# Moving the streamed operands of a split-fp32 kernel to other places modulo 512 bytes

## The chip, the cores and the metric

The kernel runs on one core of a Trainium2 chip. The metric is the device time of one execution in microseconds. The kernel before took 1244.25 us (median of 3 runs, 1238.74 to 1244.99).

## The reference, cut to what matters

Two transformer-like blocks over 256 tokens of width 1024. Nearly all the work is products of activations with large fp32 weight matrices:

```python
proj = h @ w_in[l]                        # 8192 columns, then conv / attention / retention mixers
up   = einsum('bsnw,nwd->bsnd', branches, w_branch[l])
x    = x + merged @ w_o[l]
x    = x + memory_attention(h, mem_n, w_xq[l], w_xkv[l], w_xo[l])
x    = x + square(relu(h @ w_up)) @ w_down
# second block: state-space mixer, then latent attention, each followed by
h    = layer_norm(ALPHA * h + mix)
h    = layer_norm(ALPHA * h + (silu(g) * val) @ down)   # g, val = split(conv(h @ up))
```

## The kernel before, in words

**Split products.** Each operand is kept as a hi part, rounded to the type `fp32r`, and a lo part, the rest. A product is three matmuls into the same PSUM bank (`mm3`): hi by hi, hi by lo, lo by hi, in the order lhsT hi / rhs hi, lhsT hi / rhs lo, lhsT lo / rhs hi. Each matmul has a stationary operand, loaded into the array by a weight load, and a moving operand, which streams past it. The weight load of a matmul is issued while the matmul before it streams.

**Weights.** All weight matrices come as 204 chunks of at most 1 MB in the order of use (`chunk_plan`). A chunk is read into the ring `wr` (two slots of 8 KB per partition), ScalarE copies it into the ring `wh` (hi, four slots), VectorE subtracts to give `wl` (lo, four slots). A planner (`Plan`, `tick`, `split_next`) decides while the program is written at which place in each engine's order these steps stand; it looks at modelled times, not at addresses.

**Two forms of product.** In `wstat` the weights are stationary (128 columns, 512 bytes per partition) and the transposed activations stream past them, 256 columns (1024 bytes) per matmul: tiles `ah`/`al` from `new_act`, `br`, `memT`, `cT`. In `xstat` the activations are stationary and weights stream past them, 512 columns (2048 bytes) per matmul, in the tail of some products too; `wmixed` does the same with 256 columns. `ah`/`al`, `memT` and `cT` are used in both forms; `mt`, `oT`, `gT`, `yT` only in `xstat`.

**Places.** Tiles are placed in SBUF by the order in which pools open: DMA scratch (16,384 bytes per partition), constants, `acts`, small pools, the rings of the weights, then one pool per stage; `memT` and `mt` lie in a pool on the right side. Adding up the tile sizes gives these places modulo 512 bytes in the kernel before:

| tile | place mod 512 | minus the place of the weights |
|---|---|---|
| `wh`, `wl` | 288 | 0 |
| `ah`, `al`, `mt`, `memT` | 480 | 192 |
| `cT` (behind a gap of 704), `oT` of the latent attention | 480 | 192 |
| `br`, `gT`, `yT`, `oT` of the memory attention, its `kT`, `qs`, `v` | 288 | 0 |

A weight chunk's slices begin at multiples of 512 bytes in its slot, save in a few narrow chunks: `dt` has 32 columns (128 bytes) per row block, `kvq` 704 columns. Below, the *offset* of a matmul is the place of what streams minus the place of what is loaded next to it, modulo 512. It is 192 for `ah`, `al`, `memT`, `cT` in `wstat`, 0 for `br`, and 320 (that is, minus 192) where weights stream past tiles at 192.

The order of instructions around the change is set by the planner alone. All instructions are recorded under line 284 (the helper `call` of `Lane`), so groups are told apart by tile names.

Of the kernel before, what the change touches and what calls it, by code (L numbers as in the profile page):

```python
# [6 lines left out]
F32 = mybir.dt.float32  # L7
F32R = mybir.dt.float32r
# [8 lines left out]
P = 128  # L17
D = 1024
S = 256
ALPHA = 4 ** 0.25  # L20
NG = 8
RAW, HELD = 2, 4
# [440 lines left out]
        self.sync = Lane(plan, nc.sync, "sp")  # L463


class Kern:
    def __init__(self, nc, tc, a, dbg=None):
        self.at = Plan()
        self.nc, self.tc, self.a, self.dbg = Engines(nc, self.at), tc, a, dbg
        self.plan, _ = chunk_plan()  # L470
        self.nch = len(self.plan)
        self.n_dma = self.n_prep = self.n_half = self.n_get = self.n_done = 0
        self.raw, self.held, self.subs = {}, {}, []
        self.bg = []
        self.floor = 0.0
        self.turns = {}
        self.blocked, self.table = False, None
        self.work = self.skew = 0.0
        self.sums = np.concatenate([[0.0], np.cumsum([len(ks) * max(n, P) * UNIT for _, ks, _, n, _ in self.plan])])

# [334 lines left out]
        self.nc.sync.dma_start(out=t, in_=self.a["prow"][0:1, o + c0:o + c0 + n].to_broadcast([P, n]))  # L815
        return t

    def new_act(self):

        return (self.acts.tile([P, 8, S], F32R, tag="ah", name="ah"), self.acts.tile([P, 8, S], F32R, tag="al", name="al"), [0, 0])  # L820

    def ready(self, act, k, *taus):
        if len(act) == 3:
# [113 lines left out]

    def gap(self, pool, n):

        pool.tile([P, n // 4], F32, tag="gap", name="gap")  # L940

    def pair(self, pool, name, n):
        return tuple(pool.tile([P, n, S], F32R, tag=name + x, name=name + x) for x in "hl")

    def mm1(self, out, lhsT, rhs, start):
        self.nc.tensor.matmul(out, lhsT=lhsT, rhs=rhs, start=start, stop=True, skip_group_check=True)
# [9 lines left out]
    def mixers(self, act):  # L956
        nc, a = self.nc, self.a
        mp, mp_close = self.open("mix")
        br = self.pair(mp, "br", 12)
        gt = Slots(self, mp, "gt", [P, 3, S], F32, 4)  # L960
        r256 = Slots(self, mp, "r256", [P, 256], F32, 6)
        hb = mp.tile([P, 24], F32, tag="hb", name="hb")
# [260 lines left out]
        ap_close()  # L1223
        rp, rp_close = self.open("merged", side="right")
        mt = self.pair(rp, "mt", 8)
        memT = self.pair(rp, "memT", 8)
        gm = self.bcast("mem", self.gb, "gb")
        g_mem = self.spawn(self.mem_norm(gm, memT))
        for m in range(8):
# [27 lines left out]
    def memory(self, x, mt, memT, mt_close):  # L1257
# [4 lines left out]
        oT = self.pair(mp, "oT", 8)  # L1262

        kT = (mp.tile([P, 8, S], F32R, tag="kT", name="kT"), mt[1])
        qs = Slots(self, mp, "qs", [P, 2, 2, S], F32R, 2)

        pTs = [tuple(k[:, 2 * h:2 * h + 2, :] for k in kT) for h in range(4)]
# [423 lines left out]
    def ffn(self, layer, h, act):  # L1691
        nc = self.nc
        pool, close = self.open(f"ffn{layer}")
        gT = self.pair(pool, "gT", 22)
        r512 = Slots(self, pool, "r512", [P, 2, S], F32, 6)

        def col(t):
            c = COLS["fcw"] + 132 * layer + t
            b = COLS["fcb"] + 44 * layer + t
            return lambda j: self.pcol[:, c + 44 * j:c + 44 * j + 1], self.pcol[:, b:b + 1]  # L1700

        def up_out(j):
            def run(pt, t):
                acc = yield from r512.wait()
                gs = [self.taps(acc[:, i, :], pt[:, 256 * i:256 * i + 256], 3, *col(j + 22 * i)) for i in range(2)]
                for g in gs:
                    next(g)
                yield "dve"
                for _ in zip(*gs):
                    pass  # L1710
                self.free(pt)
                yield "act"
                nc.scalar.activation(acc[:, 0, :], acc[:, 0, :], AF.Silu)
                yield "dve"
                nc.vector.tensor_mul(acc[:, 0, :], acc[:, 0, :], acc[:, 1, :])
                yield "act"
                yield from self.split((gT[0][:, j, :], gT[1][:, j, :]), acc[:, 0, :])
                r512.put(acc)
            return run

        tasks = []
        self.wmixed("fu", act, 8, [up_out(j) for j in range(MIXED["fu"][layer])], tasks)
        self.dump(("h1", "h2")[layer], h)
        for j in range(MIXED["fu"][layer], 22):
            self.wstat("fu", act, 8, up_out(j), tasks)
        g_, b_ = self.bcast(f"lfg{layer}", self.gb, "gb"), self.bcast(f"lfb{layer}", self.gb, "gb")
        act = None if layer else self.new_act()
        ps = self.xstat("fd", [2] * 11, self.lhs(gT), [(0, 512), (512, 1024)], tail=TAIL["fd"][layer],
                        before=lambda c: self.until(*tasks[2 * c:2 * c + 2]),
                        after=lambda t, p, got: self.layernorm(t, h, g_, b_, act, p, got))  # L1730
        close()
        return act
# [32 lines left out]
    def attention(self, h, act):  # L1765
        nc = self.nc
        cos, sin = self.cs[:, 0], self.cs[:, 1]
        pool, close = self.open("mla")
        self.gap(pool, 704)
        cT = self.pair(pool, "cT", 5)  # L1770
        krT = pool.tile([P, S], F32, tag="krT", name="krT")
        knT = pool.tile([P, 8, S], F32, tag="knT", name="knT")
        qnT = pool.tile([P, 8, S], F32, tag="qnT", name="qnT")
# [194 lines left out]
    def program(self):  # L1968
        nc, tc, a = self.nc, self.tc, self.a
        cs = []  # L1970

        def pool(name, bufs=1, **kw):
            cm = tc.tile_pool(name=name, bufs=bufs, **kw)
            cs.append(cm)
            return cm.__enter__()

        cp = pool("const")
        self.gb = pool("gb", 2)  # L1980
        self.dram = pool("dram", space=bass.MemoryType.DRAM)
        self.acts = pool("acts")
        cq = pool("small")
        self.tiny = pool("tiny", 4)
        self.tk = Slots(self, pool("tk"), "tk", [P, D], F32, 2)
        self.wraw, self.whi, self.wlo = pool("wraw", RAW), pool("whi", HELD), pool("wlo", HELD)
        pp = pool("ps", space=PSUM)
        self.mm = Slots(self, pp, "mm", [P, 512], F32, 4)
        self.sm = Slots(self, pp, "sm", [P, 512], F32, 4)

        x = cp.tile([P, 2, D], F32, tag="x", name="x")
        self.cst = cst = cq.tile([P, NCST], F32, tag="cst", name="cst")
        self.ones = cp.tile([P, P], F32, tag="ones", name="ones")
        nc.vector.memset(self.ones, 1.0)

        row = self.tk.get()
        o, w = ROWS["mix"]
        nc.sync.dma_start(out=row[0:1, :], in_=a["prow"][0:1, o:o + w])
        halves = [slice(512 * n, 512 * n + 512) for n in range(2)]
        for c in halves:  # L2000
            nc.sync.dma_start(out=x[:, 0, c], in_=a["x"][0:P, c])
        nc.sync.dma_start(out=cst[:, 0:P], in_=a["cst"][:, 0:P])
        self.pump(1)
        nc.sync.dma_start(out=x[:, 1, :], in_=a["x"][P:2 * P, :])
        self.pump()
        nc.sync.dma_start(out=cst[:, P:], in_=a["cst"][:, P:])
        gs = [self.mm.get() for c in halves]
        for pt, c in zip(gs, halves):
            self.mm1(pt, self.ones[0:1, :], row[0:1, c], True)
        self.tk.put(row)  # L2010
        self.pcol = cp.tile([P, NCOL], F32, tag="pcol", name="pcol")
        nc.sync.dma_start(out=self.pcol, in_=a["pcol"])
        self.ident, self.nu, self.ut = (cst[:, CST[n]:CST[n] + P] for n in ("ident", "nu", "ut"))
        self.at.one = cq.tile([1, 2], F32, tag="one", name="one")
        nc.vector.memset(self.at.one, 1.0)
        self.neg1 = cp.tile([P, P], F32, tag="neg1", name="neg1")
        nc.vector.memset(self.neg1, -1.0)
        self.mhalf = cq.tile([P, 2], F32, tag="mhalf", name="mhalf")
        nc.vector.memset(self.mhalf, -0.5)
        self.identb = cp.tile([P, P], BF16, tag="identb", name="identb")  # L2020
        nc.vector.tensor_copy(self.identb, self.ident)

        self.maskb = cp.tile([P, P], BF16, tag="maskb", name="maskb")
        nc.vector.memset(self.maskb, 0.0)
        nc.gpsimd.affine_select(out=self.maskb, in_=self.maskb, compare_op=ALU.is_ge, fill=-1e30, base=0,
                                pattern=[[-1, P]], channel_multiplier=1)

        act = self.new_act()
        self.until(self.spawn(self.rms(0, x, Halves(gs), act), first=True))

        def second():
            yield from self.rms(1, x, Halves(gs), act)
            for pt in gs:
                self.mm.put(pt)

        self.spawn(second(), first=True)
        mt, memT, mt_close = self.mixers(act)
        self.spawn(self.angles(cp))
        act, close = self.memory(x, mt, memT, mt_close)
        act = self.mlp(x, act, close)  # L2040
        act = self.ssd(x, act)
        act = self.ffn(0, x, act)
        act = self.attention(x, act)
        self.ffn(1, x, act)
        self.drain()
        assert self.n_get == self.nch
        for cm in reversed(cs):
            cm.__exit__(None, None, None)
# [21 lines left out]
```

## Time and profile before

| | |
|---|---|
| runs before | 1244.99, 1238.74, 1244.25 us |
| profiled execution | 1244.83 us; span of its instructions 1243.1 us |
| TensorE matmul busy | 1224.7 us of the span (99%), 8468 matmuls |
| VectorE / ScalarE busy | 853.9 us (69%) / 717.0 us (58%) |
| DMA engines | 182 GB/s read from HBM over the span |
[...]

A matmul's end in these records is modelled. What counts is the distance from start to start, the pace: the number of matmuls in a stretch without idle time gives it. A group's mean duration is a steady amount longer than its pace.

### The profile page before, as it was taken

The page shows a single profiled execution, that of the slowest core. Times are in us where ns is not written, and L with a number is a line of the kernel's source. Part 1 is how long each engine was busy: PE and PEld are TensorE (multiplying, and loading weights), DVE is VectorE, ACT ScalarE, POOL GpSimd, SP SyncE. Part 2 cuts the span into 40 slices and gives each one's busy share as a digit, 9 for nine tenths or more (in the row PEclk, how much of TensorE's full clock was granted, in tenths as well). Part 3 has the DMA queues.
Part 4 walks back from the last instruction along what each step waited for, and adds up shares of the span by engine and source line. Part 5 has one row for each costly group of instructions (what it writes and reads, how often), then busy time and mean ns, then how long its engine had stood idle before and what let it go on. Part 6 is the DMA issues. An engine that isn't in the chain of part 4 may idle for free.

```text
span 1243.1 us, 20768 instructions
## 1 busy us (share of the span) xinstructions
PE 1224.7 (99%) x8468; PEld 1120.8 (90%) x8468; DVE 853.9 (69%) x1378; ACT 717.0 (58%) x1181; POOL 53.5 (4%) x85
## 2 busy tenths in 40 slices
PE   7999999999999999999999999999999999999997
PEld 5978999989989998889999898999988888999986
DVE  5666847666746665446787797877765866888853
ACT  5666546446536554335788765666644575666641
POOL 0011000000000000000111201000000000000000
PEclk9999999999999999999999999999999999999999
DMA  7643355546544546524656555555573443455560
GB/s 254 235 167 127 146 196 219 179 156 228 176 152 159 214 172 221 201 106 166 227 190 233 193 174 194 187 172 202 184 259 118 161 181 123 172 197 182 213 256 35
DMA packets 35425, 227.71 MB, mean 183 GB/s; under 512 B 4321, under 2 KB 4993, under 8 KB 11522
## 3 DMA queue, kind: packets, MB, share of 16 engines
q1 hardware_dynamic: 35330, 226.39, 50.8%
q8 instruction: 66, 1.08, 0.4%
q14 instruction: 29, 0.24, 0.1%
HBM read 225.27 MB, written 1.10 MB: 182 GB/s over the span
## 4 chain that ended last, share of the span: by engine, by line
PE 95%; DVE 3%; DMA 1%; issue 0%; ACT 0%; POOL 0%; SPq 0%; POOLq 0%; DVEq 0%; ACTq 0%
PE mm L284 85%; PE sm L284 9%; DVE wl L284 1%; DVE x L284 1%; DMA wr<-wts 0%; DVE tk L284 0%; DMA cst<-cst 0%; POOL rs L284 0%; ACT wh L284 0%; DVE ln L284 0%; DVE al L284 0%; SPq L284 0%; POOLq L2066 0%; ACT r L284 0%; ACT ah L284 0%
## 5 line engine op out<-in xcount | busy, mean ns | idle before, releaser
L284 DVE TENSOR_TENSOR wl<-wr,wh 128x1024 fp32r<-128x1024 f32 (+3 forms) x408 | 479.4, 1198 | 173.7 <-ACT wh L284 173.0
L284 ACT CAST wh<-wr 128x1024 fp32r<-128x1024 f32 (+3 forms) x408 | 403.6, 1029 | 162.4 <-PE mm L284 87.9
L284 PE MATMUL mm<-ah,wh 128*128 128x256 f32 (+1 forms) x1496 | 421.1, 281 | 0.0
L284 PE MATMUL mm<-ah,wl 128*128 128x256 f32 (+1 forms) x1496 | 417.5, 279 | 0.0
L284 PE MATMUL mm<-al,wh 128*128 128x256 f32 (+1 forms) x1496 | 417.4, 279 | 0.0
L284 PEld LDWEIGHTS mm<-ah,wh 128*128 128x128 f32 (+1 forms) x1496 | 283.0, 189 | 1.6 <-issue 1.1
L284 PEld LDWEIGHTS mm<-ah,wl 128*128 128x128 f32 (+1 forms) x1496 | 281.0, 188 | 0.1
L284 PEld LDWEIGHTS mm<-al,wh 128*128 128x128 f32 (+1 forms) x1496 | 280.5, 188 | 0.4
L284 DVE SCALAR_TENSOR_TENSOR r<-mm,pcol,r 128x255 f32<-128x255 f32 (+2 forms) x212 | 86.9, 474 | 38.6 <-ACT r L284 38.6
L284 PE MATMUL mm<-wl,ah 128*128 128x512 f32 (+3 forms) x320 | 106.3, 338 | 3.1 <-DVE wl L284 3.0
L284 PE MATMUL mm<-wh,ah 128*128 128x512 f32 (+3 forms) x320 | 108.6, 345 | 0.0
L284 PE MATMUL mm<-wh,al 128*128 128x512 f32 (+3 forms) x320 | 105.9, 337 | 0.5 <-DVE al L284 0.5
L284 PE MATMUL mm<-wh,gTh 128*128 128x512 f32 x304 | 96.3, 391 | 0.0
L284 PE MATMUL mm<-wh,gTl 128*128 128x512 f32 x304 | 95.6, 389 | 0.0
L284 PE MATMUL mm<-wl,gTh 128*128 128x512 f32 x304 | 95.6, 390 | 0.0
L284 ACT ACTIVATE r<-mm,pcol 128x256 f32<-128x256 f32 x96 | 48.9, 560 | 46.9 <-PE mm L284 46.9
L284 PEld LDWEIGHTS mm<-wl,ah 128*128 128x128 f32 x320 | 60.3, 189 | 10.2 <-DVE wl L284 4.9
L284 PEld LDWEIGHTS mm<-wh,gTl 128*128 128x128 f32 x304 | 57.1, 188 | 11.8
L284 PEld LDWEIGHTS mm<-wl,gTh 128*128 128x128 f32 x304 | 57.1, 188 | 11.8
L284 PEld LDWEIGHTS mm<-wh,gTh 128*128 128x128 f32 x304 | 56.7, 188 | 12.0 <-issue 0.6
L284 PEld LDWEIGHTS mm<-wh,al 128*128 128x128 f32 x320 | 60.3, 189 | 7.0 <-DVE al L284 1.1
L284 PEld LDWEIGHTS mm<-wh,ah 128*128 128x128 f32 x320 | 60.3, 189 | 6.6 <-issue 0.7
(296 smaller groups left out, 1581.8 us busy)
## 6 DMA issues: line engine op xcount, KB each, us to landing
wr<-wts SPq DMA_DIRECT2D x186, 1024.0 KB, 4.9
wr<-wts SPq DMA_DIRECT2D x11, 768.0 KB, 4.3
gb<-prow SPq DMA_DIRECT2D x12, 512.0 KB, 6.8
dec<-rows SPq DMA_DIRECT2D x8, 768.0 KB, 7.5
wr<-wts SPq DMA_DIRECT2D x4, 704.0 KB, 4.2
wr<-wts SPq DMA_DIRECT2D x4, 512.0 KB, 7.0
tk<-mem SPq DMA_DIRECT2D x2, 512.0 KB, 7.9
out<-x SPq DMA_DIRECT2D x4, 256.0 KB, 2.1
```

Source lines behind the costliest of these rows:

```text
L284: r = f(*args, **kw)
```

## The change

`PLACE = (448, 320)`: hi and lo parts of operands that stream past weights are put 448 and 320 bytes (mod 512) behind the place of the weights. This is done with padding: `new_act` allocates 128 columns more and slices; `stream` replaces `pair` for `br`, `memT`, `cT` and puts gap tiles around them. A gap of 192 bytes ahead of the weights' rings moves these from 288 to 480, so that everything in stage pools without a gap now stands at the weights' own place: `mt`, `oT`, `gT`, `yT`, and the activation for `kvq` (`new_act(False)`). In the memory attention a gap of 64 puts `qs` and `v` 64 bytes behind `kT` and `mt`, which stream past them: offset 448. The DMA scratch shrinks from 16 KB to 1 KB, which makes the room. No instruction is added, removed or resized.

```diff
+PLACE = (448, 320)
...
-    def new_act(self):
-
-        return (self.acts.tile([P, 8, S], F32R, tag="ah", name="ah"), self.acts.tile([P, 8, S], F32R, tag="al", name="al"), [0, 0])
+    def new_act(self, stream=True):
+
+        h, l = (self.acts.tile([P, 8 * S + 128], F32R, tag=n, name=n)[:, (at if stream else 0) // 4:][:, :8 * S]
+                .rearrange("p (k s) -> p k s", s=S) for n, at in zip(("ah", "al"), PLACE))
+        return (h, l, [0, 0])
...
     def gap(self, pool, n):
 
-        pool.tile([P, n // 4], F32, tag="gap", name="gap")
+        self.n_gap += 1
+        pool.tile([P, n // 4], F32, tag=f"gap{self.n_gap}", name="gap")
...
+    def stream(self, pool, name, n):
+
+        self.gap(pool, PLACE[0])
+        h = pool.tile([P, n, S], F32R, tag=name + "h", name=name + "h")
+        self.gap(pool, (PLACE[1] - PLACE[0]) % 512)
+        t = h, pool.tile([P, n, S], F32R, tag=name + "l", name=name + "l")
+        self.gap(pool, -PLACE[1] % 512)
+        return t
...
-        br = self.pair(mp, "br", 12)
+        br = self.stream(mp, "br", 12)
...
-        memT = self.pair(rp, "memT", 8)
+        memT = self.stream(rp, "memT", 8)
...
+        self.gap(mp, 64)
         qs = Slots(self, mp, "qs", [P, 2, 2, S], F32R, 2)
...
-        act = None if layer else self.new_act()
+        act = None if layer else self.new_act(False)
...
-        self.gap(pool, 704)
-        cT = self.pair(pool, "cT", 5)
+        cT = self.stream(pool, "cT", 5)
...
-        self.wraw, self.whi, self.wlo = pool("wraw", RAW), pool("whi", HELD), pool("wlo", HELD)
+        self.gap(pool("gap0"), 192)
+        self.wraw, self.whi = pool("wraw", RAW), pool("whi", HELD)
+        self.wlo = pool("wlo", HELD)
...
-    nc = bacc.Bacc("TRN2", target_bir_lowering=False, num_devices=1)
+    nc = bacc.Bacc("TRN2", target_bir_lowering=False, num_devices=1, dynamic_dma_scratch_size=1024)
```

The offsets after: `wstat` 448 when a hi part streams (two of three passes), 320 when a lo part does; `xstat` and `wmixed` past tiles that also stream 64 and 192; past all others 0.

## Rows read from the trace of the kernel before

**Rows 1.** The page: span, busy time by engine, the granted clock in 40 slices, the chain that ended last by engine.
```profile
span 1243.1 us, 20768 instructions
PE 1224.7 (99%) x8468; PEld 1120.8 (90%) x8468; DVE 853.9 (69%) x1378; ACT 717.0 (58%) x1181; POOL 53.5 (4%) x85
...
PEclk9999999999999999999999999999999999999999
...
PE 95%; DVE 3%; DMA 1%; issue 0%; ACT 0%; POOL 0%; SPq 0%; POOLq 0%; DVEq 0%; ACTq 0%
```

**Rows 2.** PE alone in stretches that hold one kind of product: start and end in us, length, busy time and number of matmuls (those that reach over an edge count too), granted clock, DMA share, GB/s. 236 to 244 is `br`; 500 to 540 is `gT` with 512 columns; the others are `ah`/`al` or (274 to 294) `memT` with 256 columns.
```profile
28.00:44.00 16.00, 16.00 (x138) 1.00 0.61 215
142.00:180.00 38.00, 38.00 (x337) 1.00 0.59 208
236.00:244.00 8.00, 8.00 (x69) 1.00 0.52 187
274.00:294.00 20.00, 20.00 (x174) 1.00 0.58 211
400.00:460.00 60.00, 60.00 (x512) 1.00 0.54 193
500.00:540.00 40.00, 40.00 (x179) 1.00 0.51 185
796.00:890.00 94.00, 94.00 (x800) 1.00 0.53 181
1080.00:1165.00 85.00, 85.00 (x753) 1.00 0.54 186
```

**Rows 3.** Groups of PE by shape: the lo pass of `al` in 1080 to 1165 and in 795 to 890, and `gT` (hi) in 500 to 540. Count, busy us, mean ns of one, idle.
```profile
L284 PE MATMUL mm<-al,wh 128*128 128x256 f32 x251 | 69.4, 276 | 0.0
L284 PE MATMUL mm<-al,wh 128*128 128x256 f32 x270 | 76.0, 281 | 0.0
L284 PE MATMUL mm<-wh,gTh 128*128 128x512 f32 x60 | 18.5, 389 | 0.0
```

**Rows 4.** The timeline of PE at the chunk `dt` (first and last lines; 24 matmuls whose weight loads are 32 columns): start, busy, instruction.
```profile
570.99 0.28 PE L284 MATMUL mm<-ah,wh 128*32 128x256 f32 x1
571.10 0.28 PE L284 MATMUL mm<-al,wh 128*32 128x256 f32 x1
571.22 0.28 PE L284 MATMUL mm<-ah,wl 128*32 128x256 f32 x1
571.34 0.28 PE L284 MATMUL mm<-ah,wh 128*32 128x256 f32 x1
571.45 0.28 PE L284 MATMUL mm<-al,wh 128*32 128x256 f32 x1
...
573.61 0.28 PE L284 MATMUL mm<-ah,wl 128*32 128x256 f32 x1
573.72 0.28 PE L284 MATMUL mm<-ah,wh 128*128 128x256 f32 x1
```

**Rows 5.** The timeline of PE where weights of 512 columns stream past `ah`/`al` (offset 320), first and last line of ten.
```profile
640.70 0.40 PE L284 MATMUL mm<-wh,ah 128*128 128x512 f32 x1
...
642.81 0.40 PE L284 MATMUL mm<-wh,ah 128*128 128x512 f32 x1
```

**Rows 6.** The whole run by shape: the groups that the change touches.
```profile
L284 PE MATMUL mm<-ah,wh 128*128 128x256 f32 x1488 | 418.9, 281 | 0.0
L284 PE MATMUL mm<-ah,wl 128*128 128x256 f32 x1488 | 415.3, 279 | 0.0
L284 PE MATMUL mm<-al,wh 128*128 128x256 f32 x1488 | 415.2, 279 | 0.0
...
L284 PE MATMUL mm<-wh,al 128*128 128x512 f32 x144 | 57.3, 398 | 0.5 <-DVE al L284 0.5
...
L284 PE MATMUL mm<-wh,al 128*128 128x256 f32 x144 | 40.2, 279 | 0.0
...
L284 PE MATMUL mm<-brh,wl 128*128 128x256 f32 x96 | 27.2, 283 | 0.0
...
L284 PE MATMUL mm<-memTl,wh 128*128 128x256 f32 x64 | 17.7, 277 | 0.0
...
L284 PE MATMUL mm<-cTl,wh 128*128 128x256 f32 x40 | 11.1, 278 | 0.0
...
L284 PE MATMUL mm<-wh,mtl 128*128 128x512 f32 x32 | 10.6, 393 | 0.0
...
L284 PE MATMUL sm<-kT,qs 128*128 128x256 f32 x32 | 6.3, 280 | 0.0
...
L284 PE MATMUL mm<-wh,ah 128*128 128x384 f32 x16 | 5.4, 336 | 0.0
```

**Rows 7.** The chain in order of time, the longest pieces without a break in the second and third large stages of `wstat` (start, length, what).
```profile
794.54 154.47 PE mm L284 x1110
1073.74 161.40 PE mm L284 x1158
```

**Rows 8.** What PE waited for: total us, times, longest.
```profile
PE sm L284 <- DVE tk L284: 3.1, 1, 3.1
PE mm L284 <- DVE wl L284: 3.0, 3, 2.0
PE mm L284 <- DMA tk<-prow: 2.4, 1, 2.4
```

More of the change, by code (lines that the diff above doesn't have):

```diff
@@ L477, in __init__ @@
         self.blocked, self.table = False, None
+        self.n_gap = 0
         self.work = self.skew = 0.0
```

## The prediction

> **What bounds the kernel now.** [...] What PE waited for adds up to some 10 us, most of it at the start [rows 8]. So time is matmuls times pace, and the question is the pace.
>
> The pace comes from stretches without a break. A stretch of length T holds n matmuls of which the first reached in from outside, so pace = (T + mean duration) / n. With 256 columns streaming there are three values [rows 2, 3]: (85.00 + 0.276) / 753 = 113.3 ns; (94.00 + 0.281) / 800 = 117.9 and, likewise, 117.8 in 400 to 460 and 118.0 in 28 to 44; (8.00 + 0.283) / 69 = 120.0 for `br`. With 512 columns, past `gT`: (40.00 + 0.389) / 179 = 225.6 by the count, 226 to 227 ns as one or two matmuls over the edge are allowed for: twice 113.3, to within that. The mean duration is the pace plus 163 ns each time (276, 281, 283, 389), so means of groups can be read as paces: clean is 276.5 at 256 columns (69.4 us / 251) and 389 at 512.
>
> What sets the value? Offset 0 with 256 columns (`br`): always 120. Offset 192: 113.3 in 142 to 180, 274 to 294 and 1080 to 1165, 117.8 in 28 to 44, 400 to 460 and 796 to 890 [rows 2]. The last of each are the same code at the same addresses in the two feed-forward layers. So the place doesn't decide the pace alone: at 192 two paces are open, and something at the entry of an unbroken chain picks one, which then holds for 60 to 100 us. Offset 320 with 512 columns gives (642.81 - 640.70) / 9 = 234.4 ns at its worst [rows 5] against 227 at offset 0. At `dt` the weight loads are a quarter as wide; after a few matmuls the pace is (573.72 - 571.45) / 20 = 113.5 ns, while the offset runs through 192, 64, 448 and 320 as the narrow slices move on by 128 bytes [rows 4]. So 113.3 is where the stream itself ends up when the load hardly disturbs it, and 4.5 or 6.7 ns more is what load and stream do to each other.
>
> **The change part by part.** No instruction comes or goes; the planner's order depends on modelled times and not on addresses, so I take the order as unchanged. The sum is made against the profiled execution, 1244.8 us (span 1243.1), 0.6 above the median of the runs.
>
> [...]
>
> *Activations past weights, 192 to 448 / 320.* 3 x 1488 = 4464 matmuls [rows 6]. The lo pass is never the first of a chain, so its mean holds no waits: 415.2 / 1488 = 279.0, against 276.5 clean: 2.5 ns. Times 4464: 11.2 us over the clean pace. (With the means of all three passes, 281.5, 279.1, 279.0, it is 15 us; the difference sits in the pass that starts chains and holds waits.) What will the pace be at 448? No 128-column load at 448 is in the trace. [...] At 448 itself there are only the `dt` rows, at 113.5, with narrow loads; 320 at 256 columns has a mean of 279 [rows 6], in between. I take 113.3, the pace that most offsets can reach: gain 11.2.
>
> *`br`, 0 to 448 / 320.* 3 x 96 matmuls, 27.2 / 96 = 283.3: 6.8 ns above clean, 2.0 us. [...]
>
> *`memT`, `cT` and the heads of the memory attention.* 192 at 0.5 ns, 120 at 1.5, 96 at 3.5 to 5.5 [rows 6]: 0.1 + 0.2 + 0.4 = 0.7 us.
>
> *Weights past `mt` and the latent `oT`, 320 to 0.* 96 + 96 matmuls at 393 against 389 at offset 0 [rows 3, 6]: 0.7 us. Here the row for the new place is in the trace.
>
> *Weights past tiles that also stream, 320 to 64 and 192.* 3 x 144 with 512 columns at 398 and 3 x 144 with 256 at 279, and some 140 past `memT` and `cT`. The only rows with 64 are half of `kvq`, where 384 columns take 336, that is 173 ns against 1.5 x 113.3 = 170: not clean, no worse than 320. I take 0. Bounds: all clean, 432 x 9 + 432 x 2.5 + 140 x 5 = 5.7 us gained; all at the worst rows (234.4 and 120), 432 x 4.2 = 1.8 us lost, and about 1 more with 512 columns.
>
> *DMA scratch, gap tiles, other waits on a tile's room.* Nothing on the path that I can see; POOL issues no DMA, and PE's waits are 10 us in all, so this is bounded by a us or two.
>
> *Is the gain passed on?* VectorE and ScalarE must make weights faster. They do so now: 1158 matmuls from 1073.74 run without a break at 113.3, as the 1110 from 794.54 do at 117.8 [rows 2, 7]. That cover is there in the dense stages; without it the gain of the slow ones would turn into waits for `wl`.
>
> Sum: 11.2 + 2.0 + 0.7 + 0.7 = 14.6 us; 1244.8 - 14.6 = 1230.2, say **1230 us**. With the bounds of the fifth part and the 15 instead of 11.2 it is 1220 to 1236.
>
> **The rivals.**
> *Two paces stay.* 448 / 320 may, like 192, leave two paces open, drawn anew at each entry. Then only `br` and the 0.7 are sure: about 1242, and by how the stretches of 60 to 110 us fall (one of 100 us is worth 100 x 4.5 / 117.8 = 3.8 us) 1236 to 1250. For it: the two feed-forward layers. Against: at offset 0 there is one pace only, so some places fix it.
> *No effect of place.* Load and stream never meet, and the three paces have another cause, such as the other engines' traffic: 1244.8. The equal code of the two layers with its two paces leaves a little room for that; `br`, at 120 in every stretch, little. [...]
> *The new place is worse.* The hi part stands 64 bytes from offset 0, the one place where the pace is always slow. [...] All at 117.8: the mean pace of activations past weights is now 279.0 - 163 = 116.0, so 4464 x 1.8 = 8.0, less 0.6 for `br`, plus 312 x 4 = 1.2 for `memT` and `cT`: 1253. Hi passes at 120 and lo passes at 117.8, mean 119.3: 4464 x 3.3 = 14.7, `br` 0.2 less, the others 1.7 more: 1261. It decides from a mean pace of 116.0 on; `dt`, clean at 448 itself, speaks against, and so do the clean 512-column rows at offset 0.
> [...]
>
> **How the numbers follow.** Clean pace nearly everywhere: 0.48, 1220 to 1236. Two paces stay: 0.24. No effect: 0.03. Worse: 0.16, half of it below 1256. Below 113.3: 0.09. Differences within 0.5%, about 6 us, can hardly be told from no change: that is 1238 to 1250.5. Faster: 0.48 + 0.09 + 0.03 of the second case = 0.60; same 0.21 + 0.03 = 0.24; slower 0.16. The range 1220 to 1256 holds 0.48 + 0.27 + 0.08 = 0.83; the likeliest case alone has 1220 to 1236.
>
> **What would show it.** Right: in the stretches of `up` and both feed-forward layers the mean of all three passes is 276 to 277; `br` falls from 283 to 276; past `mt` 389; PE's waits don't grow. Wrong: a mean of 281 or 283 in any long stretch (two paces, or the worse place), a mean under 275 (below 113.3), or new waits of PE for `wl` where the pace did fall. The prediction falls if the hi passes stay within 3 ns of the 283 that `br` had before.

## The result: 1.0% slower, and the profile after

The changed kernel takes 1254.03 us (median of 4 runs, 1253.90 to 1254.29), the kernel before 1242.45 beside it (4 runs, 1238.74 to 1244.99): a ratio of 1.0096, 95% interval 1.0066 to 1.0125. The time lies inside the range, but it moved to the other side: 14.6 us of gain were forecast, and 9.2 to 11.6 were lost (by the spans of the profiled executions and by the medians).

The page of the kernel after: span, busy time, granted clock, the chain that ended last by engine, and what PE waited for (total us, times, longest).
```profile
span 1252.3 us, 20769 instructions
PE 1234.3 (99%) x8468; PEld 1128.8 (90%) x8468; DVE 854.4 (68%) x1378; ACT 716.7 (57%) x1181; POOL 53.2 (4%) x85
...
PEclk9999999999999999999999999999999999999999
...
PE 93%; DVE 3%; DMA 1%; issue 1%; POOL 0%; ACT 0%; SPq 0%; POOLq 0%; DVEq 0%; ACTq 0%
```
```profile
PE mm L284 <- DVE wl L284: 3.2, 4, 1.9
PE mm L284 <- DMA tk<-prow: 2.4, 1, 2.4
PE sm L284 <- DVE tk L284: 2.3, 1, 2.3
```
Against [rows 1, 8] the span is 9.2 us longer, and PE's busy time 9.6 (1234.3 against 1224.7) for the same 8468 matmuls at the same granted clock (0.998 on average in both). Waits are as before. The loss is in the pace alone, so it is read from stretches without a break and from the means, as in the prediction.

PE of the kernel after in stretches of one kind of product (start and end in us, length, busy, number of matmuls, clock, DMA share, GB/s): gates, `br`, `up`, `gT`, both feed-forward layers.
```profile
142.00:180.00 38.00, 38.00 (x325) 1.00 0.58 199
236.00:244.00 8.00, 8.00 (x70) 1.00 0.65 219
400.00:460.00 60.00, 60.00 (x512) 1.00 0.54 197
500.00:540.00 40.00, 40.00 (x178) 1.00 0.55 195
800.00:890.00 90.00, 90.00 (x767) 1.00 0.51 177
1080.00:1160.00 80.00, 80.00 (x682) 1.00 0.52 183
```
With the working of the prediction the paces are (38 + 0.281) / 325 = 117.8 ns, (8 + 0.281) / 70 = 118.3 for `br`, then 117.7 in `up` and in both feed-forward layers. The gates and the second layer stood at 113.3 before [rows 2]: the stretches that were clean no longer are, those at 117.8 stay there. Weights past `gT`, whose offset stays 0, keep their pace: 178 matmuls in 40 us for 179, a mean of 389 ns before and after.

Whole-run groups of PE after the change (count, busy us, mean ns of one, idle).
```profile
L284 PE MATMUL mm<-ah,wh 128*128 128x256 f32 x1488 | 420.7, 283 | 0.0
L284 PE MATMUL mm<-al,wh 128*128 128x256 f32 x1488 | 418.3, 281 | 0.0
L284 PE MATMUL mm<-ah,wl 128*128 128x256 f32 x1488 | 416.6, 280 | 0.0
...
L284 PE MATMUL mm<-wh,al 128*128 128x512 f32 x144 | 57.1, 397 | 0.5 <-DVE al L284 0.5
...
L284 PE MATMUL mm<-wh,al 128*128 128x256 f32 x144 | 39.9, 277 | 0.0
...
L284 PE MATMUL mm<-brh,wl 128*128 128x256 f32 x96 | 26.9, 280 | 0.0
...
L284 PE MATMUL mm<-memTl,wh 128*128 128x256 f32 x64 | 18.1, 282 | 0.0
...
L284 PE MATMUL mm<-cTl,wh 128*128 128x256 f32 x40 | 11.3, 282 | 0.0
...
L284 PE MATMUL mm<-wh,mtl 128*128 128x512 f32 x32 | 10.5, 390 | 0.0
```
The largest group rose where it should have fallen (281 for `ah` past `wh`, 279 for the other two before [rows 6]), `memT` and `cT` rose by 4 to 5 ns, `br` fell by 3, `mt` by 3, and `wmixed` (weights of 256 columns past activations) by 2.

From the distances start to start one can add up how far each class lies above the clean pace. That pace is taken as 113.3 ns for 256 columns and in proportion for other widths (226.7 for 512); distances are cut off at 7.5 ns more, so that waits don't count, and products that are not split are left out. In us:

```
class                                before   after
activations past weights (ah, al)     11.65   19.86
br                                     1.84    1.27
memT                                   0.11    0.83
cT                                     0.21    0.56
weights of 512 past ah, al             1.69    2.21
weights of 256 past ah, al (wmixed)    1.75    0.65
weights past mt                        0.27    0.12
all split products                    20.28   28.18
```
The whole is 7.9 us of the 9.2, and `ah` and `al` alone lose 8.2 in the term that was to give 11.2. Without the cut-off the sum over all distances is 9.2 us, 9.1 of it where `ah` and `al` stream.

### The profile page after: what moved, and what is told of

Its sections match the earlier page's. It is cut to its first block, busy times and chain, and to the rows that moved or that the text cites. A ratio compares the mean times of both kernels' runs of the same rounds, so it can differ in the third digit from the quotient of the medians.

```text
span 1252.3 us, 20769 instructions
## 1 busy us (share of the span) xinstructions
PE 1234.3 (99%) x8468; PEld 1128.8 (90%) x8468; DVE 854.4 (68%) x1378; ACT 716.7 (57%) x1181; POOL 53.2 (4%) x85
## 4 chain that ended last, share of the span: by engine, by line
PE 93%; DVE 3%; DMA 1%; issue 1%; POOL 0%; ACT 0%; SPq 0%; POOLq 0%; DVEq 0%; ACTq 0%
PE mm L284 84%; PE sm L284 9%; DMA wr<-wts 1%; DVE wl L284 1%; DVE x L284 1%; DVE tk L284 0%; POOL rs L284 0%; DVE ln L284 0%; SPq L284 0%; DVE al L284 0%; ACT wh L284 0%; ACT ah L284 0%; POOLq L2083 0%; ACT r L284 0%; DVEq L2083 0%
```

## The experiments

The question is what about (448, 320) is worse than 192. The theory: a hi and a lo place fix the pace as a pair, through how the stream and the weight load beside it meet. Its rivals: being near offset 0, the sign of the distance, the moved weights or the smaller DMA scratch, or luck at the entries. Six kernels measure paces alone; the others are the whole kernel with other places. In the tables below an *excess* is (pace in ns x 2.4) minus the columns, from the tenth matmul of a chain to its last (the granted clock is 1.00 in all of them): for 256 columns 16 is 113.3 ns, 26.6 is 117.8, 32 is 120.0. The factor 2.4 only makes a scale, whose unit is called a cycle in one of the expectations; no run here shows how long a cycle of the clock is.

### The pace by place, 64 pairs

A kernel that holds only chains of 12 x 3 matmuls (12 triples, a triple being the three matmuls of one split product); every chain has its own pair of places and one of three things ahead of it, its *entry*:
```diff
+        for h, l in COMBOS:                      # 0, 64 .. 448 each
+            for kind in ("transposes", "wide", "both"):
+                enter(kind)
+                ...
+                for k in range(12):
+                    ...
+                    mul(o, wh[:, w], ah[:, sh], k == 0, False)     # sh starts at h bytes
+                    mul(o, wh[:, w], al[:, sl], False, False)      # sl at l bytes
+                    mul(o, wl[:, w], ah[:, sh], False, k == 11)
```


> A kernel of its own, which leaves out the whole computation: chains of 36 matmuls in the order of the split product (weights stationary with 128 columns, 256 columns streaming past), no other engine at work, for all 64 pairs of places of the hi and the lo part (0 to 448 in steps of 64 bytes, relative to the weights), each entered in three ways: behind four transposes, behind three matmuls with 512 columns, behind both. Theory 1, place: the pace is set by the pair alone or by pair and entry; (448, 320) gives 117.8 ns at every entry, (192, 192) 113.3 or 117.8 by entry, (0, 0) 120, and some pairs give 113.3 at every entry. Theory 2, traffic: with no other engine at work all pairs run at one pace, 113.3.

The timeline of PE in three chains, (256, 256), (448, 320) and (448, 448): the tenth matmul and the last of each, 26 apart.
```profile
559.06 0.28 PE L48 MATMUL mm<-ah,wh 128*128 128x256 f32 x1
...
562.18 0.28 PE L48 MATMUL mm<-ah,wl 128*128 128x256 f32 x1
...
934.97 0.28 PE L48 MATMUL mm<-ah,wh 128*128 128x256 f32 x1
...
938.03 0.28 PE L48 MATMUL mm<-ah,wl 128*128 128x256 f32 x1
...
965.03 0.28 PE L48 MATMUL mm<-ah,wh 128*128 128x256 f32 x1
...
967.98 0.28 PE L48 MATMUL mm<-ah,wl 128*128 128x256 f32 x1
```
(562.18 - 559.06) / 26 = 120.0 ns, as `br` had at 0. (448, 320): (938.03 - 934.97) / 26 = 117.7. (448, 448): (967.98 - 965.03) / 26 = 113.5, with times rounded to 10 ns. So the three paces of the kernel before are there with VectorE and ScalarE idle and 1 GB/s of DMA beside PE (the page of this run, from its second slice to its last). The excess of the quarter of the table that is enough (the other three repeat it: adding 256 to either place changes nothing beyond 1, or 0.4 ns, save for the first chain of the program, whose first matmuls are slower (213 ns from start to start between 14.81 and 16.09 us), and one entry at (192, 0)), for the three entries:

```
hi \ lo      0              64             128            192
  0       - /32/32     26.6/26.6/26.6  26.1/26.6/26.6  26.7/26.7/26.9
 64    29.0/30.0/30.0  26.6/26.7/26.6  26.5/26.5/26.5  26.6/26.6/26.6
128    31.1/29.4/29.4  23.9/23.8/24.8  29.0/29.0/32.0  35.5/26.6/33.9
192    30.3/26.6/26.6  26.6/26.6/26.6  29.3/29.4/28.8  16.0/26.6/16.0
```
The period is 256 bytes and not 512, so 448 is 192 and 320 is 64. For the activations the change kept the hi parts where they had been, and moved only the lo parts, from a pair that has two paces to one that has the slow one alone. Which of its two paces that pair takes goes by the entry here: at all four pairs that are (192, 192) modulo 256 it is the clean one behind transposes and behind both, the slow one behind the wide matmuls.

### The same with 512 columns

```diff
-                    mul(o, wh[:, w], ah[:, sh], k == 0, False)
+                    mul(o, ah[:, sh], wh[:, w], k == 0, False)     # w: 512 columns
```
(and so for the other two; eight triples, two entries).

> The same with the roles turned, which again leaves out the whole computation: the 128-column tiles stationary at the 64 pairs of places, 512 columns of weights streaming past at place 0, 24 matmuls a chain, entered behind four transposes or behind six matmuls with 256 columns. Theory 1: (0, 0) gives 226.7 ns, (192, 192) 229 to 234, (448, 320) 229 to 234 with a pattern over the three passes. Theory 2: all pairs at 226.7.

Only (0, 0) is clean there (excess 32, 226.7 ns); all others lie at 37 to 52 (229 to 235 ns), (192, 192) at 37.3 to 37.9, (192, 64) at 37.3. It repeats after 256 bytes too, though some entries at (0, 192), (128, 0) and (192, 0) differ by 2 to 4 (0.8 to 1.7 ns). So of these places the form with weights streaming is fastest at offset 0, where the form with activations streaming takes 32 (120.0 ns), near the slow end; that form is clean at (192, 192) alone.

### The pair mirrored, and the pair of before

```diff
-PLACE = (448, 320)
+PLACE = (64, 192)
...
-        self.gap(mp, 64)
+        self.gap(mp, -PLACE[0] % 512)
```


> The whole kernel with hi and lo parts at 64 and 192 in place of 448 and 320: the same distances to the other side. In the changed kernel, weights with 256 columns streaming past tiles at 448 and 320 see just these offsets, 64 and 192, and run clean there. Theory 1 with the sign as the cause: activations past weights fall from a mean of 281 to about 276.5, 5184 matmuls by 4.4 ns, so 1254 - 23 = 1231 us, give or take 3 for the weights that now stream past tiles at offsets 448 and 320. Rival, any place near 0 is bad: mean 281 to 283, 1252 to 1262. Rival, place is not the cause: 1254.

1253.47 us (5 runs, 1252.81 to 1253.97), a ratio of 1.0067 to the kernel before, 1.0044 to 1.0091 (1243.77 in 8 runs beside it). Its stretches of `up` and the two feed-forward layers:
```profile
400.00:460.00 60.00, 60.00 (x512) 1.00 0.54 197
800.00:890.00 90.00, 90.00 (x766) 1.00 0.51 178
1080.00:1160.00 80.00, 80.00 (x682) 1.00 0.51 182
```
The 1231 us of the first theory didn't come. The counts are those of the change to within one, as 26.6 at (64, 192) in the table says. For this pair the sign plays no part; that it never does isn't shown, and in the table (64, 64) is slow at every entry where its mirror (192, 192) is not.

The same two lines with `PLACE = (192, 192)`: the weights, the gaps and the DMA scratch of the change, and the offset of `ah` and `al` before, now for `br` as well.

> One part of the change alone: the weights and all that does not stream move as in the change, and so do br and cT, but everything that streams stands at 192, hi and lo, as the activations did before. Theory 1: two paces again, 1236 to 1246 us with a spread over the runs like before, br at 276 or 281 instead of 283. If it is as slow as the change (1254 with little spread), not the places 448 and 320 but something else in the change (DMA scratch, gaps) costs the time.

1236.72 us (4 runs, 1236.18 to 1236.81), 0.993, 0.9905 to 0.9955. What the change does besides choosing its pair costs nothing, and with `br` at 192 it gives a little. The wide spread that was expected didn't come: the runs lie within 0.6 us. Two of its stretches, slow and clean:
```profile
28.00:44.00 16.00, 16.00 (x138) 1.00 0.64 232
...
400.00:460.00 60.00, 60.00 (x532) 1.00 0.59 211
```

### One number of the change undone

```diff
-PLACE = (448, 320)
+PLACE = (448, 448)
```


> The changed kernel with one number changed: lo parts at 448 instead of 320. Modulo 256 the pair is then (192, 192) instead of (192, 64). If the pace has a period of 256 bytes and the pair decides, the two paces come back: 1236 to 1246 us, long stretches at a mean of 276 or 281 ns, none held at 281 everywhere. If the place of the hi part at 448 was the fault, or 448 is not the same as 192, the time stays at 1254.

1235.9 us (7 runs, 1235.55 to 1236.75), 0.9966, 0.9955 to 0.9978 (1240.56 in 16 runs beside it). Its stretches and groups:
```profile
28.00:44.00 16.00, 16.00 (x138) 1.00 0.62 225
...
236.00:244.00 8.00, 8.00 (x73) 1.00 0.52 157
...
400.00:460.00 60.00, 60.00 (x532) 1.00 0.59 208
...
800.00:890.00 90.00, 90.00 (x797) 1.00 0.55 196
1080.00:1160.00 80.00, 80.00 (x708) 1.00 0.55 198
```
```profile
L284 PE MATMUL mm<-ah,wh 128*128 128x256 f32 x1488 | 415.7, 279 | 0.0
L284 PE MATMUL mm<-ah,wl 128*128 128x256 f32 x1488 | 412.2, 277 | 0.2 <-DVE wl L284 0.2
L284 PE MATMUL mm<-al,wh 128*128 128x256 f32 x1488 | 412.1, 277 | 0.0
...
L284 PE MATMUL mm<-wh,al 128*128 128x256 f32 x144 | 40.2, 279 | 0.0
```
532 for 512, 797 for 767, 708 for 682: the place of the lo part alone is worth 1254.0 - 1235.9 = 18 us (16 by the two ratios to the kernel before). As with (192, 192), the time came out at the lower end of what was expected, with little spread. The hi part still stands at 448, 64 bytes from offset 0, so nearness to 0 isn't the cause; and as (448, 448) takes the time of (192, 192), the period of 256 holds in the whole kernel. `wmixed` is back at the 279 of before: the 2 ns that it gained came from the lo part's new place.

### Luck at the entries

In 72 entries (0 to 5 transposes and 0 to 5 wide matmuls, in both orders) for each of three pairs:
```diff
-ENTRIES = ("transposes", "wide", "both")
+ENTRIES = [(t, w, o) for t in range(6) for w in range(6) for o in (0, 1)]
...
-COMBOS = [(h, l) for h in range(0, 512, 64) for l in range(0, 512, 64)]
+COMBOS = [(192, 192), (192, 64), (0, 0)]
```


> What picks the pace (leaves out the whole computation): chains of 36 narrow matmuls at the pairs (192, 192), (192, 64), (0, 0), entered behind 0 to 5 transposes and 0 to 5 wide matmuls in either order. (192, 64) stands for the change, 448 and 320 being 192 and 64 modulo 256. Theory 1: (0, 0) at 120 ns and (192, 64) at 117.8 at every entry, (192, 192) at 113.3 or 117.8 by entry and at nothing else. If entry is what decides at every place, (192, 64) also shows 113.3 somewhere, and the change was only unlucky.

(192, 192) behind two transposes and one wide matmul, in the one order and in the other; the tenth matmul and the last:
```profile
142.04 0.28 PE L48 MATMUL mm<-ah,wh 128*128 128x256 f32 x1
...
144.99 0.28 PE L48 MATMUL mm<-ah,wl 128*128 128x256 f32 x1
...
146.61 0.28 PE L48 MATMUL mm<-ah,wh 128*128 128x256 f32 x1
...
149.67 0.28 PE L48 MATMUL mm<-ah,wl 128*128 128x256 f32 x1
```
2.95 / 26 = 113.5 ns and 3.06 / 26 = 117.7. Of all entries:

(192, 64): 27 at all 72. (0, 0): 32 at all 72. (192, 192): 16 at 37 of them, 27 at 34, nothing between (the program's first chain is left out). Without transposes ahead, all ten entries behind wide matmuls took the slow pace; with transposes it was 36 clean to 24 slow, and no rule in their number that I could find. In a later sweep, below, (192, 192) took the clean pace behind three wide matmuls, so what stood further ahead counts too. The chains that end clean reach it by the sixth matmul; the others are slow to their end. Two paces, picked in the first matmuls of a chain and held, are thus a property of that pair and not of the stage or of the other engines. That the runs of the kernel before spread over 6 to 8 us and those of the change over 0.4 would fit this, as the change has nothing to draw, but it isn't shown: one execution of each kernel has a trace, and the two kernels with (192, 192) and (448, 448) can draw too and spread over 0.6 and 1.2 us.

A last kernel is the kernel before with every tile 192 bytes further on, all offsets kept:
```diff
+        self.gap(pool("gap0"), 192)
         cp = pool("const")
...
         memT = self.pair(rp, "memT", 8)
+        self.gap(rp, 320)
...
```


> The kernel before with every tile moved on by 192 bytes mod 512 (gap of 192 ahead of the constants, one of 320 behind memT in the pool on the right, DMA scratch 1 KB); every offset of the kernel before stays as it was: 192 for ah, al, memT, cT, 0 for br, 320 past mt and oT. Theory A (only offsets count, the pace at 192 is drawn anew at entries, and what is at 0 or 320 costs the same): ratio 0.998 to 1.002, runs spread over 1238 to 1246 like the kernel before, some long stretches at 117.8 ns. Theory B (the two kernels with (192, 192) and (448, 448) ran steadily at 1236 because their tiles stand at other absolute places): runs within 1 us of each other, at 1238 to 1239.5 (1236 and 2.7 us for br, mt and oT), the long stretches all at 113.3 ns.

1240.25 us (12 runs, 1238.82 to 1246.96) against 1240.39 (17 runs, 1238.47 to 1246.56): 0.9998, 0.9981 to 1.0015. Theory A holds; this move of the absolute place counts for nothing, median and spread are the same. Its draw in the profiled execution:
```profile
28.00:44.00 16.00, 16.00 (x144) 1.00 0.68 244
...
400.00:460.00 60.00, 60.00 (x512) 1.00 0.56 202
...
800.00:890.00 90.00, 90.00 (x767) 1.00 0.53 188
1080.00:1160.00 80.00, 80.00 (x708) 1.00 0.54 196
```
Clean at 28 to 44, where the kernel before drew the slow pace (138 [rows 2]), and otherwise the same draws. What stays open is why the two kernels with both parts at 192 or 448 run so steadily (11 runs within 1.3 us). In their traces the long stretches are clean, while 28 to 44 is slow in both (138 matmuls). Their `br` stands at 192 instead of 0, so that no stretch at 120 ns lies among the others; whether that is what steadies them wasn't tried.

### Looking for a pair without the draw

Steps of 16 bytes, modulo 256, with 10 triples and two entries:
```diff
-COMBOS = [(h, l) for h in range(0, 512, 64) for l in range(0, 512, 64)]
+COMBOS = [(h, l) for h in range(0, 256, 16) for l in range(0, 256, 16)]
```


> The narrow sweep again (it leaves out the whole computation), now over 256 bytes in steps of 16, as the first sweep repeated itself every 256 bytes: 256 pairs, chains of 30 matmuls, entered behind four transposes and behind three wide matmuls. If only the distance to the nearest bad place counts, the paces between the steps of 64 lie between those of their neighbours and no place is clean at both entries. If the pattern is finer, some pairs are at 113.3 ns (16 cycles over 256) at both entries, and the kernel can be placed so that no entry falls into the slow pace: by the counts of before, some 11 us less than 1243.

Most of the 256 pairs lie between 24 and 33 (116.7 to 120.4 ns) and nothing can be interpolated: neighbours of a slow pair are now slower, now faster. (112, 112) alone is clean (17) at both entries, (0, 0) is at 32. So the whole kernel with `PLACE = (112, 112)`:

> The changed kernel with hi and lo parts at 112, the pair that was clean at both entries of the sweep in steps of 16 bytes. If the sweep holds in the whole kernel, all activations past weights run at a mean of 276 to 277 ns at every entry: the 6.4 us that the kernel with 192 still loses there are gone, 1230 us, give or take 2 for weights streaming past tiles at 112, which no sweep has shown, and with a small spread. If the places of the weights' slots or other engines matter as well, some stretches are at 281 and it lands at 1236 to 1245.

1241.1 us (10 runs, 1240.38 to 1243.05), 0.9997, 0.9983 to 1.0011. No gain where 1230 was expected; two stretches and two groups of it say why:
```profile
236.00:244.00 8.00, 8.00 (x69) 1.00 0.45 158
...
400.00:460.00 60.00, 60.00 (x532) 1.00 0.54 194
```
```profile
L284 PE MATMUL mm<-al,wh 128*128 128x256 f32 x1488 | 410.5, 276 | 0.0
...
L284 PE MATMUL mm<-wh,al 128*128 128x256 f32 x144 | 40.8, 283 | 0.0
```
`ah` and `al`, each a slice of a wider tile, are clean: 276. But tiles of their own were put at multiples of 32 bytes, so a gap of 112 left `br` at 128 (69 matmuls in 8 us, as at offset 0) and `mt` 32 bytes off its place (395 and 400 ns). And `wmixed`, now past tiles at 112, rose from 279 to 283.

One more measurement of paces: 50 entries at (112, 112) and at (192, 208), and both parts together in steps of 8 bytes, for both forms of product:
```diff
+        for h in range(0, 256, 8):
+            ...
+                    s = slice(h // 4 + 256 * q, h // 4 + 256 * q + 128)
+                    mul(o, ah[:, s], wh[:, w], k == 0, False)
```


> Chains alone (leaves out the whole computation): the pairs (112, 112) and (192, 208) behind 50 entries each; then equal places from 0 to 248 in steps of 8, with 512 columns streaming at two entries and with 256 columns at three. If (112, 112) is clean whatever the entry, all 50 chains are at 113.3 ns; if the sweep only met two lucky entries, some are at 117.8. With 512 columns only places near 0 should be at 226.7.

(112, 112) lies at 16 to 19 at 49 entries (the fiftieth is the program's first chain): most of its chains start slower, all come to the clean pace by the 16th matmul and lie at 16 over their last ten. (192, 208) lies at 24 to 25, at 32 at one entry. Of the 32 places of both parts together, 16, 112, 144 and 192 reach 16 to 18 at some entry, only 112 at all of them. With 512 columns not only 0 is clean, as was expected, but 120 and 216 too (16 and 240 at one entry); 112 has 48, 192 has 37.

Then everything streamed at exactly 112 by slices, only the state-space mixer's activation at 192:
```diff
-PLACE = (448, 320)
+PLACE, SSD = 112, 192
...
+    def placed(self, pool, name, n, at=PLACE):
+
+        return tuple(pool.tile([P, n * S + 128], F32R, tag=name + x, name=name + x)[:, at // 4:][:, :n * S]
+                     .rearrange("p (k s) -> p k s", s=S) for x in "hl")
...
-        br = self.stream(mp, "br", 12)
+        br = self.placed(mp, "br", 12)
...
```


> All that streams past weights at exactly 112 (tiles with 128 columns of room and a slice, as separate tiles can only be placed in steps of 32 bytes), save the activations of the state-space mixer, past which many wide matmuls stream, at 192; all else at the weights' place as in the change. br, memT and cT fall from a mean of 282 to 284 (in the kernel with 112) to 276 to 277: 1.3 + 0.9 + 0.6 us; mt and the latent oT return to the clean 389: 1 us; so 1241.1 - 3.8 = 1237, less 0.6 for the mixer. If 192 was only lucky in its entries, this is the steadier one at 1235 to 1237; if the wide matmuls at 112 cost more than they seem to, 1238 to 1241.

1236.75 us (7 runs, 1235.02 to 1238.55), 0.9954, 0.9937 to 0.9972: where it was expected, and no better than (448, 448).
```profile
L284 PE MATMUL mm<-al,wh 128*128 128x256 f32 x1488 | 410.3, 276 | 0.0
...
L284 PE MATMUL mm<-wh,al 128*128 128x256 f32 x144 | 40.8, 283 | 0.0
L284 PE MATMUL mm<-brh,wh 128*128 128x256 f32 x96 | 26.6, 277 | 0.0
```
The long passes and `br` are clean. The sums over the clean pace, made for both kernels as above, say why that brings nothing over (448, 448): 1.4 us are gained with `ah`/`al` streaming and 0.7 with `memT`, and 0.7, 0.6 and 0.3 lost with weights past `ah`/`al` (256 and 512 columns) and past `memT`. What streams in one product stands still in another, and the two forms want different places.

### Does the load take part? Loads of 32 columns

```diff
-                    w = slice(256 * q, 256 * q + 128)
+                    w = slice(256 * q, 256 * q + 32)
```
(and the products go to 32 partitions of PSUM instead of 128).

> The narrow sweep over 64 pairs with the suspected cause taken down to a quarter: weight loads of 32 columns instead of 128, the streams unchanged (it leaves out the whole computation). If load and stream meeting in SBUF is what costs the time, most pairs are at 113.3 ns, the others nearer to it than with 128 columns, (0, 0) and (192, 64) among them. If the stream's own place against something else decides, the table stays as it was: 120 at (0, 0), 117.8 at (192, 64).

The tenth matmul and the last at (256, 256), 120.0 ns with full loads, now (559.22 - 556.16) / 26 = 117.7:
```profile
556.16 0.28 PE L48 MATMUL mm<-ah,wh 128*32 128x256 f32 x1
...
559.22 0.28 PE L48 MATMUL mm<-ah,wl 128*32 128x256 f32 x1
```

The streams stand where they stood, only the load is a quarter as wide: (0, 0) falls from 32 to 27 at most entries, (192, 64) from 26.6 to 23, (192, 192) from two paces to 16 at all three entries, (64, 64) from 26.6 to 16 at two entries and 24 at one. Most pairs lie at 21 to 27, so neither expectation came true as it stood: only 29 of the 192 chains are at 16, and the table changed nearly everywhere. Of the chains 157 got faster by more than 1, and only those at (128, 64) slower (24 or 25 to 27). So loads of 32 columns, with products on 32 partitions, mostly lessen the loss but don't take it away. Where in the chip it arises, and why some pairs pay more than others, no run shows.

## Why the prediction was wrong, point by point

**What bounds the kernel: right.** Time is matmuls times pace: PE is busy 99% of the span before [rows 1] and after, at a granted clock of 1.00 in all stretches above and in [rows 2]. The order of PE's matmuls is that of before, its waits didn't grow [rows 8], and PE's busy time grew by 9.6 us where the span grew by 9.2.

**Three paces, two of them open at 192, drawn at entry: right.** All three came out of a kernel with nothing else at work, to 0.2 ns, and the draw with them. The rival that place has no effect falls: one shape at one clock takes 113.3, 117.8 or 120.0 ns with nothing but the places and the entries changed, and with a narrower load 157 of 192 chains are faster.

**Activations past weights at 448 / 320 take 113.3 ns, gain 11.2 us: the step that failed.** They take 117.8 everywhere and the term is a loss of 8.2. The prediction's own sign of its fall came true: hi passes within 3 ns of the 283 that `br` had, now at 283 and 280. Two things were wrong in it. The only rows at 448 were those of `dt` [rows 4], whose loads are 32 columns, and I let them stand for loads of 128. Moreover hi and lo stand alike in `dt`, at 192 and then at 64 modulo 256. The runs show that with such loads these two pairs take 16, or 24 at one entry, and the change's mixed pair, (192, 64), takes 23; with full loads it takes 26.6. The reading of `dt` as "where the stream ends up when the load hardly disturbs it" is half right (some pairs do reach 16), but what it was to prove is not in it. And I took the two numbers one by one, modulo 512 as the kernel's text has it. Modulo 256 they are 192 and 64: the hi part hadn't moved, so that the only question was the lo part's 64, for which the trace had next to nothing (half of `kvq` in the other form [rows 6], and the 234.4 ns of [rows 5]). The trace of before could not show the period; it did show that there was no row for the pair, and 0.48 for the clean pace was too much for a price that rested on `dt`.

**"The new place is worse", all at 117.8: this is what happened**, with its price. It said 8.0 for `ah` and `al`, less 0.6 for `br`, plus 1.2 for `memT` and `cT`, 1253 us. Measured are 8.2, 0.6, 0.7 + 0.35, and 1254.0. Its reason was wrong: a hi part 64 bytes from 0 does no harm, as (448, 448) shows.

**`br`, a gain of 2.0: in part.** 120 became 117.8, 0.6 us; at (448, 448) the mean duration is 276 to 278 ns and 1.7 of the 2.0 us are there.

**`memT`, `cT`, heads, a gain of 0.7: wrong in sign**, by the step above; `memT` and `cT` lost 1.1, and the heads gained 0.1 where 0.4 was said.

**`mt` and the latent `oT`, 320 to 0: right in direction.** 393 became 390 for `mt` and 389 was said; this row was in the trace. By the distances the two gained 0.25 us of the 0.7.

**Weights past tiles that also stream, taken as 0, bounds 5.7 gained and 1.8 lost.** 256 columns gained 1.1, 512 lost 0.5, past `memT` and `cT` lost 0.2: a gain of 0.4 in all. The "about 1 more with 512 columns" in the bounds has no row behind it, as the mean of 398 there already is a pace of 235 ns, above the 234.4 that was called the worst; and the bounds as they are worked out end at 1233, not at 1236.

**Scratch, gaps and the moved weights, taken as 0: right**, by the kernel with (192, 192) and by the one moved on by 192 bytes.

**Below 113.3, given 0.09: falls.** No run shows a pace under 113.3 ns with 256 columns, and no row of the trace of before did: none of the pairs in any of the six kernels of paces goes under an excess of 16.

The sum that follows from the runs: (448, 448) has what the forecast meant, less the draws that stay. It is 8.1 us under the profiled execution of before in span (1235.0 against 1243.1), 6.8 of it in `ah`/`al` and 1.7 in `br`, 0.75 lost in `memT`. Part of that is the slow draw of that one execution: by the medians of runs side by side, 1240.56 and 1235.9, it is 4.7.

## What to carry to other kernels

A pace measured at one operand's place was here a price for that pair of places with that width of load: 113.3 ns for many chains at (192, 192), 117.8 at (192, 64), about 116 there with loads of 32 columns. Where a change moves operands to a place for which the trace has no row of the same shape on both sides, measure chains of the bare matmuls at that place first, at several entries, or hold the term at zero. Ask of every constant by which modulus it counts: had the period been known, (448, 320) would have read as "lo parts from 192 to 64". One piece of code at one place that shows two paces is a property with two values; a change may gain by fixing the good one or lose, as here, by fixing the bad one.

## What the runs showed of the hardware

- For `fp32r` matmuls without a break at a granted clock of 1.00 the pace depends on where the streamed operands stand against the loaded ones, modulo 256 bytes: from 113.3 to 120.0 ns for 256 columns at most pairs (up to 122 at a few), 226.7 to 235 for 512. Pairs 256 bytes apart agree within 0.4 ns for 256 columns, save one entry at (192, 0) and the program's first chain; for 512 columns some entries differ by 0.8 to 1.7 ns.
- The lowest pace seen is 113.3 ns with 256 columns and 226.7 with 512, 0.443 ns per column in both.
- At both parts 192, two paces (113.3 and 117.8) are open, one is taken in the first matmuls, the clean one at 37 and the slow one at 34 of 71 entries, and held for as long as the chain runs: 36 matmuls in the small kernel, over 700 in the large one. At both parts 112 all 49 entries end in the clean one.
- 256 columns streaming are among the slowest at offset 0, 120.0 ns in all 72 entries; 512 columns are clean there (226.7 ns) and, of 32 places in steps of 8 bytes, at every entry only at 120 and 216 besides. Loads of 32 columns instead of 128 lower 117.8 to about 116 ns at (192, 64) and 120.0 to about 118 at (0, 0) at most entries.
